# A seven-product output gate, weight sums made one stage earlier, and new scheduler times in an eight-core decoder step

## The chip, the cores and the metric

The kernel runs on the 8 NeuronCores of one Trainium2 chip, as one launch. The metric is the device time of the slowest core, in microseconds (us). A program on all 8 cores has a second, slower state in some of its executions: one die or both show a lower granted TensorE clock and the time grows by some per cent. Engines: PE is TensorE, DVE is VectorE, ACT is ScalarE, POOL is GpSimd, SP is SyncE, which here only issues DMA transfers. "PEclk" is the granted TensorE clock as a share of full speed.

## The reference

Each core takes one prompt sequence of 2048 tokens and 16 sample tokens through two layers of width 1024. An even layer (pooling and a gated recurrence), an MLP, an odd layer (the gated convolution), a second MLP:

```python
def odd_layer(h, conv_prev, w_in, conv_w, w_out):
    t_ = h.shape[1]
    bg, cg, hv = jnp.split(h @ w_in, 3, axis=-1)
    z = cg * hv                                                # C * (W_in x)
    ext = jnp.concatenate([conv_prev.astype(z.dtype), z], axis=1)   # (B, CONV_BUF + T, D_CONV)
    conv = conv_w[0] * ext[:, 0:t_]
    for j in range(1, CONV_WIDTH):
        conv = conv + conv_w[j] * ext[:, j:j + t_]
    return (bg * conv) @ w_out, ext[:, -CONV_BUF:]
# trunk, per layer:  x = x + mixed;  h = rmsnorm(x);  x = x + square(relu(h @ ff_w1)) @ ff_w2
```

`conv_prev`, the state of the convolution for the sample tokens, is 128 KB per core.

## The kernel before

All large products are fp16 on PE. Most are done by the Strassen-Winograd scheme: seven products in place of eight for a 2x2 block product, paid for with sums of blocks on DVE. In the convolution `cg` and `hv` were already done so; the output gate `bg` was done plainly, and the weight sums were made by DVE inside the stage (cut):

```python
        def conv_wsums(p):                       # in the convolution, for each half p of the tokens
            for c in range(8):                   # channel block of 128
                ...
                for i, (o, a, b, op) in enumerate((("s1", "a21", "a22", ALU.add), ("s2", "s1", "a11", ALU.subtract),
                                                   ("a21", "a11", "a21", ALU.subtract), ("s4", "a12", "s2", ALU.subtract))):
                    ...
                    yield TT(W[o][0], W[a][0], W[b][0], op, W[a][1] + W[b][1], W[o][1], fast=True)
        def conv_bg(p, c, kb):                   # output gate, plain: 2 x 8 matmuls 128x512
            W = cwts[p, c]
            for t in (2 * p, 2 * p + 1):
                ...
                yield MMG([(bank(k), W[f"bg{k8 // 4}"][0][:, (k8 % 4) * 128:(k8 % 4 + 1) * 128], hT[:, k8, tokslice(t)], k8 == 0, k8 == 7)
                           for k8 in range(8)], W["bg0"][1] + W["bg1"][1] + hTb(t), [B_ps[k]])
```

No order of instructions is written by hand. Tasks like these yield operations, and a list scheduler in Python, when the program is built, always places the operation that it reckons can start first (ties go by priority). Each engine gets its own stream in exactly that order. So a cost in this scheduler is never a cost on the chip; it only decides what stands ahead of what:

```python
HOP = 0.06                                       # reckoned time from one engine's result to another's start
TIE = 0.03
DMA_RATE = (0.30, 0.25)
DMA_FIXED = (2.0, 2.5)
    def est(self, op):
        return max(self.free[op.eng], self.ready(op) + HOP + op.margin)
    def emit(self, op):                          # ... of a DMA:
        begin = max(self.dma_free, start + op.occ)          # one pipe for all transfers of the core
        self.dma_free = begin + nbytes / (DMA_RATE[ph] * 1e6)
        done = self.dma_free + DMA_FIXED[ph] + op.lat       # op.lat: the "slack" argument of DMA()
```

One task that the change does not touch: it loads the state of the convolution, transposes it on PE into the bank `pp`, and copies it on.

```python
        def conv_state():
            yield up(*[("pgdone", p) for p in range(NPG)])
            stage = pgf(CSTAGE, 4)[0:16, :]
            yield DMA("sp", misc(), [(stage, st_conv.rearrange("b r c -> b (r c)"))], (), pgb(CSTAGE, 4), 131072)
            it = yield Alloc(SB)
            k = it[0]
            yield TRG([(bank(k)[:, i * 16:(i + 1) * 16], stage[:, i * 128:(i + 1) * 128], identf[0:16, 0:16])
                       for i in range(16)], pgb(CSTAGE, 4) + [B_small], it[1])
            yield CP(prevT[:, :, :, :], ...)
```

## Time and profile before

| | us |
|---|---|
| time before, median of 4 runs (lowest to highest) | 1422.38 (1420.93 to 1443.44, the last slow) |
| spans of the eight cores in the profiled execution | 1415.1 to 1420.7 |

The page of the slowest core, core 2: busy time of each engine, PE's and the clock's share in 40 equal slices of 35.5 us (tenths), and the chain of waits that ended last.

```profile
span 1420.7 us, 25535 instructions; the slowest of 8 cores (1415.1 to 1420.7 us)
...
PE 1377.5 (97%) x9160; PEld 698.0 (49%) x9182; DVE 1133.3 (80%) x2096; ACT 895.0 (63%) x1806; POOL 189.3 (13%) x274
...
PE   8989999999999999999999999998999999999996
...
PEclk9999999999999999999999999999999999999998
...
PE 88%; DVE 5%; DMA 2%; ACT 2%; issue 1%; SPq 0%; DVEq 0%; POOL 0%; ACTq 0%; POOLq 0%
...
```

PE is the bound: 97% busy, 88% of the chain, clock full nearly everywhere. Slices are counted from 0. After slice 2 (71 to 107 us) the one dip in PE's row before the last slice is slice 27 (959 to 994 us), where the convolution hands over to the second MLP. The next view is the table of stretches of core 2: first MLP, convolution with its output projection, second MLP.

```profile
...
core 2: us, PE busy (x) PEld busy (x) DVE busy (x) ACT busy (x) POOL busy (x), PEclk, DMA share, GB/s
409.60:774.80 365.20, 361.10 (x2201) 172.53 (x2202) 284.67 (x502) 231.68 (x447) 31.71 (x60) 1.00 0.47 79
774.80:1001.20 226.40, 217.88 (x1289) 103.21 (x1287) 201.95 (x415) 109.81 (x205) 16.41 (x31) 0.98 0.41 68
1001.20:1409.20 408.00, 407.31 (x2382) 191.47 (x2381) 318.37 (x548) 259.97 (x515) 31.17 (x59) 1.00 0.50 95
...
```

In the convolution DVE is 201.95 us busy of 226.4, 89%. There PE waits for DVE:

```profile
...
PE pp L598 <- DVE hT L558: 3.8, 2, 2.5
PE pp L598 <- ACT pp L532: 1.8, 2, 1.0
PE pp L600 <- DVE x_sb L558: 1.5, 2, 1.2
PE pp L600 <- DVE arena L586: 0.8, 1, 0.8
PE pp L598 <- DVE ring L558: 0.6, 1, 0.6
```

This is PE's timeline of core 7 around 391 us, and that core's DMA issues from 355 to 392 us (size of each, median us from issue to landing).

```profile
...
391.05 1.18 PE L610 MATMUL pp<-identf,arena 16*128 16x16 f32 x16
...
```

### The profile page before, as it was taken

What the parts mean: (1) busy time and instruction counts of PE and PEld (TensorE: products, weight loads), DVE (VectorE), ACT (ScalarE), POOL (GpSimd) and SP (SyncE); (2) the same over time, 40 slices, a digit from 0 to 9 for tenths busy, and PEclk for the clock granted to TensorE, in tenths of its full rate; (3) what the DMA queues carried; (4) which work ended last, traced back from release to release, by engine and by line L of the source; (5) the groups of instructions that cost most, each with busy time, mean ns of one, the idle gap of its engine ahead of it and who ended that gap; (6) DMA issues with size and microseconds to landing.
All of it is one profiled execution on the core that took longest, in us unless ns stands there. A gap on an engine that the chain in (4) does not pass through costs nothing.

```text
span 1420.7 us, 25535 instructions; the slowest of 8 cores (1415.1 to 1420.7 us)
## 1 busy us (share of the span) xinstructions
PE 1377.5 (97%) x9160; PEld 698.0 (49%) x9182; DVE 1133.3 (80%) x2096; ACT 895.0 (63%) x1806; POOL 189.3 (13%) x274
## 2 busy tenths in 40 slices
PE   8989999999999999999999999998999999999996
PEld 3666555654444444454445444444444544444442
DVE  5887898886677778877769999979778788977767
ACT  5868888874455656864667434455647757755655
POOL 1121134333200110010000010000100100100100
PEclk9999999999999999999999999999999999999998
DMA  8681353397644743642633644440735626644612
GB/s 187 158 134 32 89 137 92 93 203 145 153 90 74 120 73 57 109 78 46 116 53 56 101 79 72 67 83 1 126 62 96 105 43 107 163 107 74 119 31 119
DMA packets 64281, 136.68 MB, mean 96 GB/s; under 512 B 6751, under 2 KB 33598, under 8 KB 64142
## 3 DMA queue, kind: packets, MB, share of 16 engines
q0 software_dynamic: 28256, 97.07, 41.0%
q1 hardware_dynamic: 35902, 37.97, 8.7%
q8 instruction: 77, 1.26, 0.4%
q14 instruction: 46, 0.38, 0.1%
HBM read 216.61 MB, written 15.54 MB: 163 GB/s over the span
## 4 chain that ended last, share of the span: by engine, by line
PE 88%; DVE 5%; DMA 2%; ACT 2%; issue 1%; SPq 0%; DVEq 0%; POOL 0%; ACTq 0%; POOLq 0%
PE pp L598 44%; PE pp L600 43%; DMA ring<-wst 1%; PE pp L610 1%; ACT arena L532 1%; DMA x_sb<-xp 1%; DVE hT L558 1%; DVE x_sb L558 1%; DVE arena L558 1%; DVE arena L570 1%; DVE mixT L558 0%; DVE gsm L558 0%; DVE x_sb L570 0%; ACT pp L532 0%; DVE mixT L563 0%
## 5 line engine op out<-in xcount | busy, mean ns | idle before, releaser
L532 ACT ACTIVATE pp<-pp 128x512 f32<-128x512 f32 x432 | 246.4, 581 | 298.8 <-PE pp L598 204.3
L558 DVE TENSOR_TENSOR x_sb<-x_sb,pp 128x512 f32<-128x512 f32 x496 | 322.1, 682 | 92.5 <-PE pp L598 37.0
L600 PE MATMUL pp<-hT,ring 128*128 128x512 f16 (+1 forms) x1700 | 301.0, 318 | 3.8 <-ACT arena L532 1.0
L600 PEld LDWEIGHTS pp<-hT,ring 128*128 128x128 f16 x1700 | 131.6, 97 | 138.0 <-issue 6.2
L532 ACT ACTIVATE arena<-arena 128x512 f16<-128x512 f16 (+1 forms) x287 | 174.2, 623 | 13.2 <-DVE arena L1805 6.6
L532 ACT ACTIVATE arena<-pp 128x512 f16<-128x512 f32 (+3 forms) x224 | 126.9, 574 | 51.5 <-PE pp L600 25.2
L598 PE MATMUL pp<-ring,arena 128*128 128x512 f16 x480 | 120.7, 379 | 0.3
L598 PE MATMUL pp<-hT,ring 128*128 128x512 f16 x456 | 114.8, 379 | 0.6 <-ACT pp L532 0.5
L600 PE MATMUL pp<-ring,mixT 128*128 128x512 f16 x416 | 97.8, 381 | 3.2 <-DVE x_sb L558 1.7
L558 DVE TENSOR_TENSOR hT<-pp,gcols_s 128x512 f16<-128x512 f32 (+1 forms) x96 | 81.9, 862 | 15.7 <-PE pp L598 7.9
L598 PE MATMUL pp<-mixT,arena 128*128 128x512 f16 x368 | 92.9, 379 | 0.2 <-ACT pp L532 0.2
L1805 DVE CUSTOM_DVE_ANT_0 arena<-pp,ring 128x512 f16<-128x512 f32 x106 | 70.1, 683 | 27.8 <-PE pp L598 18.2
L598 PE MATMUL pp<-ring 128*128 128x512 f16 x336 | 85.9, 379 | 0.0
L558 DVE TENSOR_TENSOR arena<-arena 128x1024 f16<-128x1024 f16 (+3 forms) x112 | 70.5, 647 | 14.5 <-ACT arena L532 13.6
L615 POOL DMA_DIRECT2D ring<-w2w x46 | 24.4, 533 | 422.2 <-DVE x_sb L558 139.1
L533 ACT ACTIVATE arena<-x_sb 128x1024 f16<-128x1024 f32 x60 | 63.1, 1052 | 21.1 <-DVE x_sb L558 16.2
L615 POOL DMA_DIRECT2D ring<-wst x73 | 39.7, 550 | 269.8 <-PE pp L600 108.5
L598 PEld LDWEIGHTS pp<-ring,arena 128*128 128x128 f16 x480 | 46.3, 98 | 54.7 <-issue 1.5
L598 PEld LDWEIGHTS pp<-hT,ring 128*128 128x128 f16 x456 | 43.6, 98 | 53.8 <-issue 4.8
L600 PE MATMUL pp<-ring,hT 128*128 128x128 f16 (+2 forms) x960 | 67.5, 227 | 2.1 <-DMA ring<-wst 2.1
L600 PEld LDWEIGHTS pp<-ring,hT 128*128 128x128 f16 (+1 forms) x960 | 60.3, 98 | 8.0 <-issue 3.0
L598 PE MATMUL pp<-mixT 128*128 128x512 f16 x240 | 61.6, 379 | 0.9 <-ACT pp L532 0.9
(258 smaller groups left out, 2303.8 us busy)
## 6 DMA issues: line engine op xcount, KB each, us to landing
ring<-wst POOLq DMA_DIRECT2D x57, 512.0 KB, 7.9
ring<-w2w POOLq DMA_DIRECT2D x46, 512.0 KB, 7.7
ring<-w1w POOLq DMA_DIRECT2D x45, 512.0 KB, 7.5
x_sb<-xp SPq DMA_DIRECT2D x28, 512.0 KB, 6.4
yp<-x_sb SPq DMA_DIRECT2D x16, 512.0 KB, 2.7
extra<-w1w POOLq DMA_DIRECT2D x15, 512.0 KB, 7.4
extra<-w2w POOLq DMA_DIRECT2D x14, 512.0 KB, 10.2
x_sb<-st_hgrn SPq DMA_DIRECT2D x24, 256.0 KB, 4.1
```

The source lines that it names most:

```text
L532: return e.activation(out=out, in_=in_, func=func, bias=bias, scale=scale)
L533: return e.activation(out=out, in_=in_, func=func, bias=bias, scale=scale, accum_out=accum)
L558: return Op(eng, lambda e: e.tensor_tensor(out=out, in0=in0, in1=in1, op=op), R, W, occ, occ + 0.08)
L570: return Op("dve", lambda e: e.scalar_tensor_tensor(out=out, in0=in0, scalar=scalar, in1=in1, op0=op0, op1=op1), R, W, occ, occ + 0.08)
L598: ins = e.matmul(o, l, r, start=s, stop=t, skip_group_check=True)
L600: ins = e.matmul(o, l, r, start=s, stop=t)
L610: ins = e.transpose(out=o, in_=i, identity=idn)
L615: fns = [(lambda e, o=o, i=i: e.dma_start(out=o, in_=i)) for (o, i) in pairs]
L1805: yield Op("dve", lambda e: e._custom_dve(TENSOR_ADD_SAT, out=v, in0=bank(k), in1=gst(n), s0=3e38, s1=0.0), [B_ps[k], B_gst[n % 2]], B, 0. ...
```

## The change

Its intent: fewer matmuls in the convolution (the gate by seven products: two channel blocks as one pair, 28 matmuls in place of 32); less DVE work there (weight sums made while the first MLP runs, stored to DRAM, loaded ready-made by the convolution; one instruction adds the shared product to two rows); and an order of instructions built from times that were measured as spacing. The core of the diff, cut:

```diff
+HOPS = {"act": 0.034, "dve": 0.034, "pe": 0.145, "pool": 0.08, "sp": 0.08}
+    def hop(self, eng):
+        return HOPS[eng] if self.late else HOP
     def est(self, op):
-        return max(self.free[op.eng], self.ready(op) + HOP + op.margin)
+        return max(self.free[op.eng], self.ready(op) + self.hop(op.eng) + op.margin)
...  # ACT; the same kind of change for DVE's operations
-                occ = 0.14 + n / 1280.0 + (0.19 if accum is not None else 0.0) + (0.0 if in_psum(in_) else 0.03)
+                occ = n / 1200.0
+                lat = occ + ((0.155 if in_psum(out) else 0.17) if ps else 0.195) + (0.19 if accum is not None else 0.0)
+                occ += (0.052 if ps else 0.093) + (0.093 if accum is not None else 0.0)
...  # weights of the convolution now come from DRAM with their sums
+                    yield DMA("sp", ringw_ds[s], [(ring[:, s, 0:3584], wsc[u - U_CONV])], B_wsc[u - U_CONV], B_ring[s], 917504)
...  # in the first MLP, 12 units x 2 halves
+        def conv_presum():
+            yield up("opX")
+            for u in range(NCU):
+                for hf in range(2):
+                    yield DMA("pool", wsc_ds[0], [(st[:, 0:1024], wst[U_CONV + u, :, 1024 * hf:1024 * hf + 1024])], (), Bst[0:4], 524288)
+                    yield DMA("sp", wsc_ds[1], [(wsc[u, :, o_:o_ + 768], st[:, 0:768])], Bst[0:3], [B_wsc[u][hf]], 196608)
+                    for o, a, b, op in (("s1", "a21", "a22", ALU.add), ("s2", "s1", "a11", ALU.subtract), ...):
+                        yield TT(V[o], V[a], V[b], op, [B[a], B[b]], [B[o]], fast=True)
+                    yield DMA("sp", wsc_ds[2], [(wsc[u, :, o_ + 768:o_ + 1792], st[:, 1024:2048])], Bst[4:8], [B_wsc[u][2 + hf]], 262144)
...  # shared product to two rows at once
+        def add_g(b, k):
+            x2 = x_sb[:, b:b + 5:4, 512:1024]
+            return TT(x2, x2, bank(k).unsqueeze(1).broadcast_to([128, 2, 512]), ALU.add, B + [B_ps[k]], B)
...
-        def conv_bg(p, c, kb):
+        def conv_bgpair(p, i, u):          # gate of two channel blocks by seven products
+        def conv_prods(p, u):
+            return [pr("a11", b11), pr("a12", b21), pr("s4", b22), pr("a22", T4, up(("ct", p, 4))),
+                    pr("s1", T1, gs[0]), pr("s2", T2, gs[1]), pr("s3", T3, gs[2])]
...  # priorities, an earlier order of the last weights, a second copy of one weight sum for the output projection
```

## The prediction

> **What bounds the kernel.** TensorE. The page gives PE 97% busy, DVE 80%, ACT 63%; the chain of waits is 88% PE. In that chain sixteen 128x512 matmuls take 3.45 us, 0.216 us each. The Trainium skill ("TensorE: Matmul & The Clock Gate", Part 1) gives 215.7 ns start to start when warm; this trace agrees. Pricing every matmul by its columns at that spacing, I estimate 59 us lost between matmuls: 34 before 325 us (the change moves nothing before about 300 us), 10 from 325 to 775 us, 15 in the convolution and its output projection (775 to 1000 us), 3 or less after. Another 11 us lie behind the last matmul.
>
> The loss in the convolution is DVE's: the table of stretches shows DVE 22 to 24 of every 25 us there. PE stands 2.5, 1.2 and 1.2 us at 969 to 975 us "<-DVE hT" and "<-DVE x_sb" (weight sums, residual adds and norms queue together as the second MLP starts); the clock is 0.91 in the next slice, about 2 us more. Smaller stops lie at 772, 776, 893, 904 and 908 us.
>
> **What the change does.**
> 1. Output gate: per pair of channel blocks 32 matmuls become 28, eight pairs: 32 fewer, 32 x 0.216 = 6.9 us, all on the critical path.
> 2. DVE in the convolution: 64 weight sums go (0.335 us apart, 21 us); taps run on 1024 columns instead of 512 (32 instructions fewer, about 2 us); 16 combining adds of 0.6 us for the gate come (+10 us). Net about 13 us less on the stage's nearly full engine.
> 3. The g product is added to two rows by one instruction: 68 fewer, about 0.07 us each, 5 us of DVE.
> 4. First MLP: 96 sums of 128x256, about 0.2 us each (estimate: half the columns), 19 us of DVE where it is 75 to 85% busy; 6.3 MB loaded, 11 MB written. PE hardly waits there now.
> 5. The convolution's weights: 24 loads of 896 KB on SP's queue, 21.5 MB instead of 12.6, in roughly 150 us; that queue moved 512 KB out in 2.7 us, so it should fit, with less spare.
> 6. Reordering, a second copy of an output weight sum and earlier norm buffers aim at the stop at 969 us.
>
> **Sum.** -6.9 (products) -8 (of the stage's 15 us of stops and clock) -1 (tail, small waits) +2 (sums waiting for their loads in the in-order DVE and POOL queues during the first MLP) = -14. Predicted **1408.5 us**, range 1399 to 1419. Faster by over 2%: 0.04; within 2%: 0.94; slower: 0.02.
>
> **What would show it right.** 32 fewer 128x512 matmuls in the convolution; the second MLP starting 12 to 16 us earlier; no idle over 2 us at that hand-over and no dip of PEclk; DVE in the convolution about 83% instead of 90%; first MLP's length unchanged within 3 us, its DVE some 5 points higher.
> **Wrong.** PE waits "<-DMA ring<-wsc", or waits on DVE in the first MLP while DVE stands "<-DMA hg<-wst": the scheduler's assumed DMA time is unchanged, while 512 KB loads on POOL's queue took 5 to 13 us here, so a sum put too early blocks everything behind it.
>
> **What would make the prediction wrong.** Under 1399: the rescheduling also empties the 10 us lost around the first MLP and the whole hand-over. Over 1419: such blocking repeated 24 times at a few us each, ring slots (down to three in the second half) starving the convolution, or a new stall at the hand-over that drops the clock.

## More of the kernel before

```profile
...
ring<-w1w POOLq DMA_DIRECT2D x3, 512.0 KB, 10.3
...
arena<-st_conv SPq DMA_DIRECT2D x1, 128.0 KB, 7.2
...
```

The sixteen 16x16 transposes start at 391.05 us with no idle before them: the load had been issued at 380.85 and had landed 7.24 us later, 3 us before PE came to it.

## The result, and the profile after

The time after is 1430.93 us (median of 4 runs, 1429.85 to 1453.49, the last slow). The ratio after over before is 1.0061 with a 95% interval of 1.0038 to 1.0084. Such ratios divide the mean time of one kernel's fast runs by that of the other's from the same rounds, so they are not quite the ratio of the medians quoted. A gain of 14 us was predicted; a loss of 8.5 was measured, outside the range.

The same lines of the page after; the slowest core is now core 7, and a slice is 35.8 us.

```profile
span 1430.3 us, 25656 instructions; the slowest of 8 cores (1421.3 to 1430.3 us)
...
PE 1374.8 (96%) x9157; PEld 695.8 (49%) x9157; DVE 1128.1 (79%) x2001; ACT 906.8 (63%) x1828; POOL 185.8 (13%) x266
...
PE   7999999999699999999999999999999999999996
...
PEclk9999999999799999999999999999999999999999
...
PE 77%; DVE 12%; ACT 4%; DMA 3%; issue 2%; SPq 0%; DVEq 0%; POOLq 0%; ACTq 0%
...
```

The dip of slice 27 is gone. In its place slice 10 (358 to 393 us) shows PE at 6 tenths and the clock at 7, in front of the first MLP, where the prediction has no step. The chain followed back through that slice (start, length, what), on core 7:

```profile
...
352.06 13.06 PE pp L628 x68
...
367.05 18.15 DMA arena<-st_conv
...
385.33 1.85 PE pp L638 x16
387.19 3.52 PE pp L628 x8
...
```
```profile
...
PE pp L638 <- DMA arena<-st_conv: 11.8, 1, 11.8
...
```
```profile
...
core 7: us, PE busy (x) PEld busy (x) DVE busy (x) ACT busy (x) POOL busy (x), PEclk, DMA share, GB/s
350.00:372.00 22.00, 20.79 (x110) 9.42 (x108) 13.29 (x28) 6.30 (x14) 10.94 (x13) 1.00 0.71 124
372.00:387.00 15.00, 3.17 (x23) 2.19 (x21) 1.19 (x2) 2.70 (x5) 0.00 (x0) 0.62 0.90 199
387.00:400.00 13.00, 13.00 (x61) 6.18 (x61) 9.38 (x19) 5.41 (x10) 0.00 (x0) 0.78 0.24 94
...
```
```profile
...
ring<-w1w POOLq DMA_DIRECT2D x3, 512.0 KB, 11.9
...
arena<-st_conv SPq DMA_DIRECT2D x1, 128.0 KB, 18.1
...
```

How to read it: PE stands 11.8 us, once, because the transposes of the convolution's state are next in its stream and their 128 KB have not landed. The load took 18.15 us; before it took 7.24. None of the ready work behind these sixteen tiny ones starts in that time (that there was some is seen below, in told_late_again, where PE is busy through the same 15 us). The Trainium skill ("PSUM — Partial Sum Buffer", "Engine vs sequencer instructions") says that matmuls start and complete in program order; this stop agrees. From 372 to 387 us PE does 3.17 us of work in 15. Then come 13 us at a mean clock of 0.78, which I estimate at 13 x 0.22 = 2.9 us more. The first eight large matmuls after the stop begin at 387.19 and take 3.52 us, 0.44 us each in place of 0.216: half speed. The Trainium skill ("TensorE: Matmul & The Clock Gate", Part 1, "What's actually happening") says that the clock falls to half after an idle window of about 3.4 us. This trace agrees: by its clock record, which notes each change of the granted clock, it falls to half 2.2 to 5.4 us (mean of the eight cores 3.6) after the stop begins, and it is full again 5.3 to 7.6 us (mean 6.5) after PE goes on. Half of that mean, 3.3 us, is my estimate of what the slow clock costs a core.

The issue times of core 7, read from the trace (issue, landing, us between), show why the load is late:

| transfer | before | after |
|---|---|---|
| ring<-w1w, POOL queue, 512 KB | 364.84, 375.17, 10.33 | 361.92, 373.85, 11.93 |
| extra<-w1w, POOL queue, 512 KB | 365.87, 381.75, 15.88 | 365.83, 380.27, 14.45 |
| nhs<-x_sb, SP queue, 256 KB, before the burst | 360.82, 363.14, 2.32 | 359.12, 361.42, 2.31 |
| nhs<-x_sb, SP queue, 256 KB, in the burst | 364.78, 380.33, 15.55 | 361.95, 378.84, 16.88 |
| arena<-st_conv, SP queue, 128 KB | 380.85, 388.09, 7.24 | 367.05, 385.20, 18.15 |

Before, the load was issued when the burst of first-MLP weights was nearly over. After, it was issued in the middle of it. It landed only 2.9 us earlier, but PE came to it 17.5 us earlier (373.50, the end of the matmuls ahead, instead of 391.05).

The scheduler did this from its reckoned times, which I printed while it built each program. In the program before, it placed the load behind the burst and reckoned 16.4 us until landing. In the program after, the load came ahead of the burst, with 5.0 us until landing. A rebuild of the recorded kernel shows how that can be: there the four first-MLP loads are reckoned to start at 345.55 to 347.20 us and the small load later, at 348.43, but it is placed before them, and the "one pipe" counts transfers in the order of placing. So the scheduler put the transposes at row 675 of PE's stream instead of row 699 (rows as I counted them; counted as operations of PE's stream in the rebuild they are 411 and 426). That shift could be read from the two orders before anything ran.

Where the time went, by stages, means of the eight cores of the profiled fast executions. Stages are cut by counting the matmuls of 512 columns, and the first one starts at the core's first matmul. In brackets: every matmul priced by its columns (64 at least) at the measured dense spacing (0.216 us for 512 columns), plus the rest, idle time and slow clock. The price of the first stage, the same in both kernels, is good to some 2 us: a recount gave 371.7.

| | up to the first MLP | first MLP | convolution and projection | second MLP | tail |
|---|---|---|---|---|---|
| before | 405.0 (373.4+31.6) | 365.3 (359.7+5.6) | 226.2 (213.3+12.9) | 408.0 (405.3+2.7) | 11.6 |
| after | 419.6 (373.4+46.1) | 365.2 (358.3+6.9) | 218.5 (208.2+10.3) | 410.2 (406.4+3.9) | 11.0 |
| difference | +14.6 | -0.1 | -7.7 | +2.2 | -0.6 |

The sum is +8.4, which is the measured +8.5. All of the loss lies before the first MLP; without that stage the change gains 6.2 us in the mean core. Of the 14.6 us the stop itself is 8.8 to 11.9 on the eight cores, 10.7 in the mean; about 4 us are left, of which the estimate above gives 3.3 to the clock. The rest of the page's table, for core 2:

```profile
...
424.10:788.60 364.50, 359.64 (x2172) 171.37 (x2171) 289.17 (x536) 224.60 (x437) 38.72 (x73) 1.00 0.65 123
788.60:1007.10 218.50, 211.94 (x1290) 101.09 (x1288) 188.42 (x301) 129.94 (x239) 5.31 (x11) 1.00 0.41 118
1007.10:1417.30 410.20, 407.64 (x2388) 192.20 (x2386) 319.50 (x524) 257.12 (x515) 31.27 (x59) 1.00 0.49 94
...
```
```profile
...
PE pp L626 <- ACT pp L543: 3.0, 5, 1.1
PE pp L626 <- ACT zT L543: 1.6, 1, 1.6
PE pp L626 <- DVE hT L578: 0.7, 1, 0.7
PE pp L628 <- DVE srs L896: 0.4, 1, 0.4
PE pp L626 <- DVE mixT L578: 0.3, 1, 0.3
PE pp L628 <- DVE mixT L578: 0.2, 1, 0.2
```

In the convolution DVE has 13.5 us less to do (201.95 to 188.42), and PE's waits for it fall from 6.7 to 1.6 us. But ACT has 20 us more (109.81 to 129.94) and PE's waits for ACT rise from 1.8 to 4.6.

### The profile page after: what moved, and what is told of

It is laid out like the page before. It is cut to its first block, busy times and chain, and to the rows that moved or that the text cites. A ratio compares the mean times of both kernels' runs of the same rounds, so it can differ in the third digit from the quotient of the medians.

```text
span 1430.3 us, 25656 instructions; the slowest of 8 cores (1421.3 to 1430.3 us)
## 1 busy us (share of the span) xinstructions
PE 1374.8 (96%) x9157; PEld 695.8 (49%) x9157; DVE 1128.1 (79%) x2001; ACT 906.8 (63%) x1828; POOL 185.8 (13%) x266
## 4 chain that ended last, share of the span: by engine, by line
PE 77%; DVE 12%; ACT 4%; DMA 3%; issue 2%; SPq 0%; DVEq 0%; POOLq 0%; ACTq 0%
PE pp L626 39%; PE pp L628 37%; ACT arena L543 2%; DVE mixT L578 2%; DMA ring<-w2w 2%; PE pp L638 1%; DVE arena L578 1%; DMA arena<-st_conv 1%; ACT pp L543 1%; DVE hT L578 1%; DVE arena L596 1%; DVE x_sb L578 1%; DVE x_sb L596 1%; DVE x_sb L584 1%; DVE arena L1848 1%
## 5 line engine op out<-in xcount | busy, mean ns | idle before, releaser
L543 ACT ACTIVATE pp<-pp 128x512 f32<-128x512 f32 x456 | 259.5, 582 | 286.9 <-PE pp L626 191.7
L578 DVE TENSOR_TENSOR x_sb<-x_sb,pp 128x512 f32<-128x512 f32 (+1 forms) x392 | 292.3, 774 | 98.2 <-ACT pp L543 41.1
L628 PE MATMUL pp<-hT,ring 128*128 128x512 f16 (+1 forms) x1460 | 252.3, 310 | 1.7 <-ACT arena L543 1.0
L543 ACT ACTIVATE arena<-arena 128x512 f16<-128x512 f16 (+1 forms) x287 | 174.4, 624 | 22.2 <-DVE arena L1848 14.3
L543 ACT ACTIVATE arena<-pp 128x512 f32<-128x512 f32 (+2 forms) x224 | 130.5, 588 | 50.7 <-PE pp L628 29.5
L626 PE MATMUL pp<-hT,ring 128*128 128x512 f16 x648 | 159.9, 379 | 2.6 <-ACT pp L543 2.4
L626 PE MATMUL pp<-mixT,arena 128*128 128x512 f16 x368 | 92.4, 379 | 0.0
L578 DVE TENSOR_TENSOR arena<-arena 128x1024 f16<-128x1024 f16 (+2 forms) x98 | 61.8, 651 | 8.3 <-ACT arena L543 7.2
L543 ACT ACTIVATE x_sb<-x_sb 128x512 f32<-128x512 f32 (+3 forms) x98 | 54.1, 559 | 14.1 <-DVE x_sb L578 10.2
L628 PE MATMUL pp<-mixT,arena 128*128 128x512 f16 x240 | 61.4, 379 | 1.2 <-DVE arena L578 1.2
L626 PE MATMUL pp<-hT,mixT 128*128 128x512 f16 x240 | 61.6, 379 | 0.0
L626 PE MATMUL pp<-ring 128*128 128x512 f16 x240 | 61.6, 379 | 0.0
```

The costliest lines, as they stand in the source:

```text
L543: return e.activation(out=out, in_=in_, func=func, bias=bias, scale=scale)
L578: return Op(eng, lambda e: e.tensor_tensor(out=out, in0=in0, in1=in1, op=op), R, W, *span(0.066, 0.15, n, two))
L626: ins = e.matmul(o, l, r, start=s, stop=t, skip_group_check=True)
L628: ins = e.matmul(o, l, r, start=s, stop=t)
```

## The experiments

Theory A: the stop in front of the first MLP is the loss, and it comes from the new scheduler times alone, which put the transposes ahead of their data. Rival B: the new traffic of the weight sums makes the load slow. A later question, theory C, was why the convolution gained 7.7 us and not 14.

### Round 1: four kernels, all slow

Mean granted clocks were 0.93 to 0.965 in the profiled executions, and the kernel before was slow too (1499.08 us median). So the times decide nothing, and I read only the waits, which are not a matter of 1%.

**e1_told_late**: after, with the true landing told to the scheduler for this one load. The transposes stand at row 693 (operation 420 in the rebuild).

```diff
-            yield DMA("sp", misc(), [(stage, st_conv...)], (), pgb(CSTAGE, 4), 131072)
+            yield DMA("sp", misc(), [(stage, st_conv...)], (), pgb(CSTAGE, 4), 131072, 12.0)
```

> The changed kernel with one number altered: the scheduler is told that the conv-state load lands 12 us later than it reckons, so it puts the sixteen 16x16 transposes of that state 18 rows later in PE's order. Theory A (PE stands 10 to 12 us at these transposes, in order, for a load that takes 18 us instead of the reckoned 5, and the clock falls afterwards; that is the whole loss before the first MLP): the 12 us wait and the clock dip go, time falls by 13 to 17 us to about 1414 to 1418 us, the stretch before the first MLP's products is back at about 405 us, the other stretches are as in the changed kernel. Rival B (the extra traffic of the weight sums, or the new work in general, slows this stretch): another wait takes its place, time stays above 1425 us.

Measured: 1492.67 us, slow. The load took 18.3 us, as in after, and PE did not wait for it. The slow load alone is not the loss; a slow load with PE next in line is.

**e2_before_told_early**: before, with the opposite lie, -11.4 instead of 12.0 in the same place. The transposes move from row 699 to 682 (operation 426 to 416).

> The kernel before with one number altered: the scheduler believes that the conv-state load lands 11.4 us earlier than it reckoned, so the transposes move 17 rows earlier in PE's order; nothing of the change is in it. Theory A: PE waits for DMA arena<-st_conv some 4 to 10 us before the first MLP and the time rises by 4 to 14 us (1426 to 1436 us). Rival B (it takes the change's own traffic): no such wait, 1422 us within 2 us.

Measured: 1509.56 us, slow. The load itself took only 6.0 us, but PE came to it early and waited 5.6 us:

```profile
...
PE pp L610 <- DMA arena<-st_conv: 5.6, 1, 5.6
```

One number in the scheduler makes the stop in the old kernel, with none of the new traffic.

**e3_after_old_times**: after, with the old hop and the old costs of ACT and DVE operations put back.

```diff
     def hop(self, eng):
-        return HOPS[eng] if self.late else HOP
+        return HOP
-                occ = n / 1200.0 ...
+                occ = 0.14 + n / 1280.0 + (0.19 if accum is not None else 0.0) + (0.0 if in_psum(in_) else 0.03)
...  # and so for DVE
```

> The changed kernel with the scheduler's old instruction times and hop (products, weight sums in DRAM and all else of the change kept). In its PE order the transposes stand where they stood before (row 699, near the first MLP's first product). Theory A (it is the new times that moved the transposes early): no wait for st_conv, 1411 to 1419 us. Rival B (weight sums' traffic is the cause): the wait stays or shows elsewhere before 425 us, over 1425 us.

Measured: 1500.03 us, slow. The transposes stand at row 699 and PE does not wait for the load, with all of the change's work and traffic.

**e4_before_new_times**: before, with only the new hop and costs put in.

> The kernel before with the new scheduler times alone. Its transposes stand at row 675, as in the changed kernel. Theory A: PE waits 8 to 13 us for DMA arena<-st_conv, clock dip, 1432 to 1440 us less whatever the times gain elsewhere (0 to 6 us). Rival B: no long wait without the weight sums' traffic, 1417 to 1423 us.

Measured: 1512.18 us, slow. The transposes stand at row 675, the load took 14.3 us, and PE waited 7.9 us, without any of the change's traffic:

```profile
...
PE pp L631 <- DMA arena<-st_conv: 7.9, 1, 7.9
...
```

The four together: the stop appears with the new times and not with the old ones, whichever work is done. That is theory A, for the stop; e2 and e4 were run in the slow state alone. "The new times" must be taken whole: when the after kernel is rebuilt with only the new hop, or with only the new costs, the load stays behind the burst (transposes at operation 428 and 425). These two programs were not run.

### Round 2: the same, fast

The kernel before had a median of 1420.34 us here.

**told_late_again**: e1's kernel once more.

> The same kernel as e1_told_late, because every run of that round fell in the slow state (granted clock 0.93 to 0.96 on both dies). Theory A: 1414 to 1418 us in the fast state, no wait for st_conv, the stretch up to the first MLP's first product 404 to 408 us instead of 415 to 422. Rival B: above 1425 us.

Measured: 1416.75 us (1416.12 to 1417.47), ratio to before 0.9974 (0.9958 to 0.9990). This is 14.2 us below the median of after, which was measured in another round; against the kernel before of each round, the difference is 12.1 us (+8.5 and -3.6). The stretches of core 7 that stopped in after:

```profile
...
350.00:372.00 22.00, 20.79 (x109) 9.40 (x108) 12.24 (x21) 6.99 (x15) 10.74 (x13) 1.00 0.66 125
372.00:387.00 15.00, 15.00 (x106) 8.27 (x104) 12.83 (x23) 9.53 (x17) 0.00 (x0) 1.00 0.82 214
387.00:400.00 13.00, 13.00 (x130) 7.23 (x129) 8.20 (x14) 7.27 (x15) 0.54 (x1) 1.00 0.13 26
...
```

PE is busy 15.00 of 15 us and the clock is 1.00, while the load, issued in the same burst, still took 17.1 us. By stages: 405.0, 365.1, 218.5, 410.3, tail 11.1. The first stage is back to the 405.0 of before, and the rest is as in after. This one number repairs the change, and this kernel beats both, before by 0.1 to 0.4%.

**before_new_told**: before with the new times and the told landing, so the new times without their stop.

> The kernel before with the new scheduler times and the conv-state load told 12 us later: what the new times are worth without the wait. Theory A: no wait for st_conv; 1416 to 1423 us, so the times alone gain 0 to 6 us once the wait is out. Rival (the times help nothing by themselves): within 1 us of before, or slower.

Measured: 1428.79 us, ratio 1.0057 (1.0039 to 1.0075). My expectation missed. No wait for the load remains, but the new times make the old work slower from the first MLP on: 405.2, 367.3, 228.3, 411.3, tail 10.6.

**after_old_times_again**: e3's kernel once more.

> The same kernel as e3_after_old_times, again for the fast state: products, weight sums in DRAM and the rest without the new times. Theory A: 1412 to 1420 us, no wait for st_conv. If the new times carry the gain in the convolution: its stretch is longer than the changed kernel's 218.5 us by 2 us or more, as it was in the slow round.

Measured: 1422.44 us, ratio 1.0013 (0.9995 to 1.0031). By stages: 404.0, 365.0, 227.4, 408.9, tail 11.3. The time expected was missed; it is no faster than before although it has the cheaper products, because the convolution took 227.4 us, 18.3 of them lost. One stop makes a third of that, on core 1:

```profile
...
PE pp L621 <- DVE extra L579: 6.6, 1, 6.6
PE pp L619 <- DVE hT L579: 1.9, 2, 1.0
...
```

A DVE sum of 2048 columns, needed by a product of the second half, was placed too late. So the convolution's stage in a 2x2 table, us:

| | old times | new times, load told late |
|---|---|---|
| old work | 226.2 | 228.3 |
| new work | 227.4 | 218.5 |

In these four programs neither half gains alone; only the pair does. Each cell is one order of instructions, and e8_tie below moves the stage by 10 us with the work and the times of the best cell, so the table alone does not show that the pair is needed.

**e6_tap_on_pool**: told_late with the first tap of each convolution moved from ACT, now loaded more, to POOL, which is nearly idle there.

```diff
-                    yield ACT(D, Z[:, 0:1024], AF.Copy, BZ + BG + [B_small], BD + BA + BB, scale=w0)
+                    yield Op("pool", lambda e: e.tensor_scalar(out=D, in0=Z[:, 0:1024], scalar1=w0, scalar2=None, op0=ALU.mult),
+                             BZ + BG + [B_small], BD + BA + BB, 2.1, 2.3)
```

> told_late with the first tap of each channel block (128x1024, 1.14 us on ACT, 18 us in all) moved from ACT to POOL. Theory C (what is left of PE's stops in the convolution are waits for ACT's copies between PSUM banks, which stand behind taps and norms in ACT's order): the stretch of the convolution falls by 1 to 3 us from told_late's 218.5 us, and PE's wait for ACT pp falls from 8 us. Rival D (the stops come from DVE, 86% busy, or from the order itself): no shorter, or longer[...].

Measured: 1429.86 us, ratio 1.0063 (1.0045 to 1.0081), convolution 230.3. POOL's taps (between the bars: busy us, mean ns of one):

```profile
...
L2313 POOL TENSOR_SCALAR arena<-arena,convwf_s 128x1024 f32<-128x1024 f32 x16 | 53.5, 3347 | 107.1 <-DVE arena L578 71.5 <-DVE arena L602 33.7 <-DVE gsm L602 2.0
...
```

3.35 us each where I had told the scheduler 2.1, and 1.14 us on ACT. DVE then waited 14.1 us for POOL, and its own two-input taps went from 1282 to 1360 ns. The run gives no support to theory C, that ACT's load holds the stage, but it does not refute it, since it brought a longer chain of its own.

### Round 3: what is left

The kernel before had a median of 1421.68 us here.

**e5_presum_later**: after, with the weight sums held back until the first MLP has begun, so that none of their transfers is in the burst.

```diff
         def conv_presum():
-            yield up("opX")
+            yield up("opX", ("X", "u", 0))
```

> The changed kernel with the weight sums started only when the first MLP's first unit has been placed, so none of their loads or stores is in flight at the state load; the transposes stand as early as in the changed kernel (row 675). Theory A (the early place in PE's order is the cause, and the load is late because of the four 512 KB loads of the first MLP before it): PE still waits 7 to 11 us for st_conv, time 1425 to 1434 us. Rival B (the weight sums' own traffic makes the load late): the wait falls under 3 us, time about 1417 us.

Measured: 1429.27 us, ratio 1.0056 (1.0041 to 1.0071). PE still waited 6.6 to 9.8 us, here core 7:

```profile
...
PE pp L638 <- DMA arena<-st_conv: 8.9, 1, 8.9
...
```

The stop does not need the change's traffic. Without that traffic it is 2.3 us shorter in the mean of the cores (8.4 in place of 10.7; on single cores from 0.9 longer to 5.0 shorter). Rival B is a small part and not the cause.

**e7_new_in_conv**: told_late, with the new times in force only while the convolution is placed.

```diff
+        self.new = []
     def hop(self, eng):
-        return HOPS[eng] if self.late else HOP
+        return HOPS[eng] if self.new else HOP
...  # the costs likewise; the flag is set at the start of the convolution and cleared at its end
```

> The changed kernel, state load told 12 us later, with the new scheduler times in force only while the convolution and its output projection are being placed; the MLPs use the old ones. If the new times by themselves lengthen the second MLP (408.0 us before, 410 to 411 in every run that has them): it comes back to about 408.5 us; with the convolution at 218 to 222 us the time is 1413 to 1418 us. If what the times do to a stage is chance: the convolution is anywhere from 218 to 230 us, time up to 1428 us.

Measured: 1420.45 us (median of all; three fast runs of 1417.99, 1418.42 and 1420.45), ratio 0.9986 (0.9966 to 1.0006). The convolution took 217.7 us, the second MLP 409.9. The gain of the convolution comes with the new times there alone. Two of the three fast times lie above the 1413 to 1418 us expected. The second MLP did not fall back to the expected 408.5 although its own instructions were placed with the old ones.

**e8_tie** and **e8b_tie**: told_late with only the scheduler's tolerance for ties changed, `TIE = 0.03` to 0.05 and to 0.02. This asks how much of any such difference is the luck of one order.

> told_late with nothing changed but the scheduler's tie width, 0.05 instead of 0.03 us: same work, same instructions, another order. Theory S (the idle that is left in a stage depends on which order the greedy scheduler happens to find, more than on DVE's load): the convolution's stretch moves by 3 us or more from 218.5 us, in either direction. Theory D (DVE's lighter load set the 218.5 us): it stays within 1.5 us of it, total 1415 to 1419 us.

> told_late with the tie width at 0.02 us: a second draw of the same. Theory S: the convolution's stretch moves by 3 us or more from 218.5 us. Theory D: within 1.5 us, total 1415 to 1419 us.

Measured: at 0.05, 1453.4 us, ratio 1.0225 (1.0210 to 1.0240); the convolution took 228.6, and the two MLPs 375.0 and 420.7. At 0.02, 1419.17 us, ratio 0.9985 (0.9970 to 1.0000), convolution 218.8. So with new work and new times the convolution stayed between 217.7 and 220.3 in four orders (after and told_late, which have the same order of matmuls there; e5; e7; and 0.02), and one careless tolerance lost the gain and more. In that run, as in after_old_times_again, PE stood once for the 2048-column sum `extra`, 5.8 us.

## Why the prediction was wrong

- **The step that failed** is a missing one: "the change moves nothing before about 300 us" is true (on core 7 the first matmul in another place is at 320 us), but the sum "-6.9 (products) -8 (of the stage's 15 us of stops and clock) -1 (tail, small waits) +2" then has no term for the 300 to 410 us before the first MLP, where the new scheduler times were in force too. That term measured +14.6 us. With the load told late, the same kernel's stage was 405.0, as before: shown by told_late_again; the stop itself was made in the old work by e2 and e4. The prediction did write that "the scheduler's assumed DMA time is unchanged" and that an operation put too early "blocks everything behind it". (Its "5 to 13 us" for 512 KB loads left out the longest, 15.8 us on core 2, which is of this very burst.) It looked for that in the operations that the change adds. It happened to one that the change does not mention.
- **Products, -6.9 predicted, -5.4 measured.** 32 matmuls went, but the trace counts 25 fewer of 512 columns (5505 to 5480, on a core whose records are complete): 7 more one-matmul products with the identity, which ready a bank for a copied product, came. Net 25 x 0.216. Those seven stand in the MLPs (two and five); in the convolution's stage itself the count is 32 fewer, as predicted. Its price falls by 5.1 us only because 32 products of 128 columns, 1.7 us, which the first MLP's stage held before, now stand in it.
- **Stops and clock in the convolution, -8 predicted, -2.6 measured** (12.9 to 10.3 us). DVE's relief came as costed, 13.5 us of busy time where 13 was predicted; its share fell from 89 to 86% and not to the 83% predicted, since the stage became shorter too. The hand-over is as predicted: no dip of the clock, and no stop over 2 us; but the second MLP, said to start 12 to 16 us earlier, starts 5.9 us later on core 2, behind the stop. And PE's waits moved to ACT, +2.8 us on core 2, as the gate's products need 96 in-place copies of a bank by ACT in place of 73. That ACT is what holds the stage I have only argued; e6 did not show it.
- **First MLP, +2 predicted: right in part by luck.** The stage kept its length (365.3 to 365.2), its lost time rose 1.3 us, and the list of DVE's waits shows none for the loads of the sums (`hg<-wst`) that I feared. But the 32 small products that left the stage hid that rise, and DVE's share there rose from 78 to 79%, not by 5 points.
- **Second MLP, 0 predicted, +2.2 measured**: 1.1 us more of priced matmuls, which are the five identity products of above, and 1.2 us more lost. It was 408.9 with the old times throughout (after_old_times_again) and 409.9 with them in this stage alone (e7), so the stage's own times do not explain all of it; the cause stays open.
- **Weights from DRAM: right.** 24 loads of 896 KB landed in 5.7 us (median) and PE never waited for one in after.

Added up: -7.7 in the convolution where -14 to -15 was meant, +2.2 after it, -0.6 in the tail, and +14.6 before the first MLP. Without the stop, told_late_again measured -3.6 us; its mean core gained more than that, but its cores fall into two groups (1409.7 to 1410.7 us and 1412.1 to 1414.6), and the slowest counts.

What stays open: why the new times help the new work and hurt the old, and how much of that is the luck of one order. The stop for the sum `extra` explains a third of what after_old_times_again lost in the convolution; the rest is many small waits whose order differs in each draw.

## What to carry to other kernels

When a scheduler places instructions on in-order engines, a better estimate of one cost can make the program slower if another estimate stays wrong: the corrected times moved a DMA-waiting instruction ahead of its data. After any change of such times, compare the order of each engine's stream, and check for every instruction that waits for a DMA on the bottleneck engine how long before its turn the data lands, taking the landing time from a trace and under the real traffic. The stop here, 8.8 to 11.9 us, cost the clock as well, by the estimate above another 3.3 us.

## What the Trainium skill lacked or had wrong

- "DMA: Bandwidth & Descriptors", "Issuing engines are not separate DMA queues": it says that transfers of the SP, ACT and POOL queues share 16 engines and interleave. The page's "Queues, rings and completion order" adds that one queue's descriptors are taken in ring order and that an engine changes between queues packet by packet. Neither says how long a small load then takes behind a burst. Here 128 KB on SP's queue took 18.15 us behind eight transfers issued on both queues in the 5.7 us before it, against 7.24 us once the burst was nearly over; 256 KB stores took 2.3 us before the burst and 16.7 to 16.9 us in it; landings came nearly in order of issue across the two queues.
- "TensorE: Matmul & The Clock Gate", Part 1: it expects 13/16 of the clock on a die once three of its cores run dense matmuls. All 8 cores ran dense fp16 matmuls here at mean granted clocks of 0.989 to 0.998 in the fast profiles; the clock records of the ten fast profiles hold only full and half on every core, never 13/16. In the slow profiles of round 1 (means 0.93 to 0.965) 13/16 does stand in the records, but for part of the time: in e1_told_late for 268 us on core 0 and for 484 us on core 4. So what the page gives as lasting came only at times.
- "GPSIMD Engine Reference", "Engine selection": it gives POOL about half of VectorE's speed for two-input elementwise work and calls one-input work "roughly line-rate". The one-input fp32 tap of 128x1024 took 3.35 us on POOL, 2.6 times the 1.28 us of a two-input tap of the same size on DVE (told_late_again). The same tap took 1.14 us on ACT; the page has no comparison with ACT, the engine that it would relieve here.
